# Seven-product chunks in five of eleven up-projection pairs, woven into one stream of units

## The chip, the cores and the metric

The kernel runs on one core of a Trainium2 chip. The metric is the device time of one execution in microseconds, as the median of several runs; lower is better. A core has a matrix engine (PE), a vector engine (DVE), a scalar engine (ACT), a third elementwise engine (POOL) and queues that issue transfers (SP's for most, POOL's for those that add to what lies at their target).

## The reference

A two-layer encoder over 256 positions of width 2048. Layer 0 mixes tokens by grouped-query attention, layer 1 by a dilated window attention; each is followed by a gated MLP. Only the MLP is touched:

```python
def conv_ffn(h, w_up, conv_w, conv_b, w_down):
    u = h @ w_up                      # [256, 2048] x [2048, 11264]
    ...
    u = lax.conv_general_dilated(...) + conv_b   # depthwise, width 3, over positions
    gate, val = jnp.split(u, 2, axis=-1)
    return (jax.nn.silu(gate) * val) @ w_down    # [256, 5632] x [5632, 2048]
```

Input and output are float32. The second mixer also needs tables of position biases, which the kernel writes to DRAM during the first MLP ("bias lines").

## The kernel before

**Products of float32.** A weight tile of 128x1024 is loaded raw, and split into a high part (`wh`, ACT, L130) and the rest (`wl`, DVE, L131); activations are kept split in the same way (`xh`, `xl`). A product is three matmuls: high by high, high by low, low by high. The 256 positions are two row halves m of 128; a matmul takes one 128x128 block of activations and 512 columns of weights.

**Units.** The up-projection has 11 pairs, each a block of 512 gate columns and the block of 512 value columns that belongs to it. The contraction of 2048 is four chunks (kg) of 512 rows. A plain unit `("c", kg, i)` is one raw tile: two row blocks of the weights, both row halves, three matmuls each, 12 in all. A chunk of a pair is four such units, two of gate and two of value, 48 matmuls. Alternatively a chunk is computed as a 2x2 block product with seven products in place of eight (Winograd's form of Strassen's method): a unit `("P", kg, f)` is one of the seven, 6 matmuls, 42 for the chunk. Its weight blocks are sums of raw tiles, its activations ("forms") sums of activation blocks, and the products M1, M5, M6, M7 have to be added up afterwards with the plain sums.

**The up-projection stage.** The MLP runs in two halves (`HALVES`: pairs 0 to 5, then 6 to 10); after each half the down-projection of these columns follows. All pairs but one run as plain feeds: `project` (L150s) computes the four gate chunks, then the four value chunks, and `feed` orders the matmuls of each activation block as `wh·xh`, `wl·xh`, `wh·xl`, so that the low part is wanted by the second matmul of a unit. Pair 0 goes through `project_woven`, which puts off the chunks whose activations come late and empties the list of waiting work before its ninth unit. Pair 6, the first of the second half, has chunk 0 by seven products through `seven` and `project_pair`, at its own start, one product and one plain unit in turn; its forms are made during the first down-projection (`first_half_forms`), and its weight sums are four DVE operations (L277). In `project_pair` a unit does its matmuls on the high part first and those on the low part last.

**Work around it.** After a block's sums are complete `up_post` scales them (ACT, L629), transposes them (DVE, L630), places the blocks (POOL, ACT, DVE: L395, L397, L399), applies the convolution's taps (ACT L638, DVE L642 and L644), and for a value block the product with the gate (L652, L668) and, in chunks that the down-projection computes by seven, the forms of the result (L684 to L696). It is a generator: `step()`, called after a unit, advances the first two of the pending ones by one stage. `spare` holds `bias_lines`, advanced when fewer than two are pending.

**Order on the engines.** A scheduler turns program order into one order per engine; a split is moved ahead by 45 instructions (`AHEAD`). There are six raw slots, three pairs of split buffers (`NHL`; the down-projection adds a fourth in `wh9`/`wl9`), and eight banks of sums: 0 to 3 in turn for a pair's gate and value, 4 to 7 for everything else (`ps_tile`, in turn).

Of the kernel before, what the change touches and what calls it, by code (L numbers as in the profile page):

```python
# [35 lines left out]
def tile_encoder(ctx: ExitStack, tc: tile.TileContext, x, xT, w_a, w_ao, q_gain, k_gain, w_b, w_bo,  # L36
# [25 lines left out]
    def nm(s):  # L62
        uid[0] += 1
        return f"{s}_{uid[0]}"
# [39 lines left out]
    def drain(keep=0):  # L104
        while len(pending) > keep:
            step()
# [110 lines left out]
    def project_pair(w, n0, n1, lhs, forms, units, late, early_done, n0_done, product_done=None, tail=False,  # L217
# [66 lines left out]
        for i, (kind, kg, p) in enumerate(units):  # L284
# [47 lines left out]
            if not (product_done or lazy) or kind == "c" or p in (1, 5, 7, 4):  # L332
                step()
        return acc

    def split(hi, lo, src):
        if lo is None:
# [91 lines left out]
    def make_forms(forms, src, k, tiles):  # L429
        for p, ms, k0 in ((1, slice(0, P), k), (2, slice(0, P), k + 2), (4, slice(P, NT), k + 2)):  # L430
            forms[p] = [tuple(t[:, ms] for t in src[k0 + j][:2]) for j in range(2)]
        yield
        xs, ts, fm = tiles()
        for j in range(4):
            hi, lo = src[k + j][:2]
            nc.vector.tensor_tensor(xs[:, j], hi.bitcast(F32), lo.bitcast(F32), ALU.add)
        yield
        q1, q0, q2, q4 = xs[:, :2, :P], xs[:, :2, P:], xs[:, 2:, :P], xs[:, 2:, P:]
        s3, s1, s2, s4 = (ts[:, i].rearrange("p (a t) -> p a t", a=2) for i in range(4))

# [12 lines left out]
        put(3, 3)  # L453
# [132 lines left out]
    def ffn(l, hT, ss_in, g_next, last, side=None):  # L586
        with tc.tile_pool(name=nm("wpool"), bufs=1) as wp, tc.tile_pool(name=nm("fpool"), bufs=1) as fp:
# [66 lines left out]
                for j in range(2):  # L654
                    split(*slots[k0 + j], cv[:, j, :])

            kept, first_forms = {}, {}

            def form_tiles():
                xs, ts = (t[:, :1024].rearrange("p (j c) -> p j c", j=4) for t in ut)  # L660
                return xs, ts, [fp.tile([P, 2, NT], F32R, tag=t, name=nm("fm"), bufs=3) for t in ("cg", "cg", "cv", "cv")]

            def first_half_forms():
                yield from make_forms(first_forms, hT, 0, form_tiles)
                zero_edges()

            def glu_forms(cg, cv, fm, hh):
                nc.vector.tensor_tensor(cv, cg, cv, ALU.mult)  # L668
# [29 lines left out]
                put(6, s2)  # L698
                put(3, s4)

            kgs = list(range(4))
            for hf, (p0, p1) in enumerate(HALVES):
                slots, forms = {}, {}
                tags = iter([(hpool, k) for k in range(24)] + [(wp, k) for k in range(24, 30)])
# [6 lines left out]
                for p in range(p0, p1):  # L711
                    if p - p0 in SKG[hf]:
                        fm = forms[p - p0] = {}
                        if p - p0 == 4:
                            f2 = fp.tile([P, 4, NT], F32R, tag="tT", name=nm("ff"))
                            f1 = fp.tile([P, 512], F32R, tag="junk", name=nm("ff"))
                            fm.update({7: (f2[:, 0], f2[:, 1]), 5: (f2[:, 2], f2[:, 3]), 6: (f1[:, :NT], f1[:, NT:])})
                        fm.update({f: new_form() for f in (1, 7, 2, 5, 4, 6, 3) + (0,) * hf if f not in fm})
                        if hf:
                            for kt in range(4):  # L720
                                slots[4 * (p - p0) + kt] = [
                                    tuple(t[:, kt % 2 * P:(kt % 2 + 1) * P] for t in fm[f])
                                    for f in ((1, 0), (2, 4))[kt // 2]]
                    else:
                        slots.update({4 * (p - p0) + j: new_form() for j in range(4)})
                    def new_tiles():
                        return ([fp.tile([P, 2, NT], F32, tag=t, name=nm(t), bufs=3) for _ in range(2)]
                                for t in ("cg", "cv"))

                    def after(hh, cg, cv, slots=slots, forms=forms, kg=p - p0):  # L730
# [4 lines left out]
                    if hf == 1 and p == p0:  # L735
                        sums = [wp.tile([P, 2, 512], F32, tag=t, name=nm("ms")) for t in ("wh9", "wl9")]
                        c = [("c", k, 2 * n + i) for n in range(2) for k in kgs[1:] for i in range(2)]
                        units = c[:2]
                        for i, f in enumerate(ORDER):
                            units += [("P", 0, f)] + c[2 + i:3 + i] * (i < 5)  # L740
                        units += c[7:]
                        cs = []

                        def gate_ready(a, p=p):
                            cs.extend(new_tiles())
                            start(up_post(a, p, cs[0]))

                        def value_ready(a, p=p, after=after):
                            start(up_post(a, NPAIR + p, cs[1], partial(after, cg=cs[0], cv=cs[1])))

                        seven(w_up[l], p, NPAIR + p, hT, lambda kg: first_forms, units,
                              [[t[:, i] for i in range(2)] for t in sums], gate_ready, value_ready)
                        continue
                    cg, cv = new_tiles()
                    after = partial(after, cg=cg, cv=cv)
                    if p == 0:
                        def gate_done(a, cg=cg):
                            taps()
                            start(up_post(a, 0, cg))

                        va = project_woven(w_up[l], p, NPAIR + p, hT, WOVEN, 4, gate_done)
                    else:
                        start(up_post(project(w_up[l], p, hT, kgs), p, cg))
                        va = project(w_up[l], NPAIR + p, hT, kgs)
                    start(up_post(va, NPAIR + p, cv, after))
# [362 lines left out]
    scr1 = dpool.tile([16, P, 256], F32, name="scr1")  # L1128

    def bias_lines(wp, lp):  # L1130
        if True:
            of = lp.tile([P, 2, 512], F32, tag="tT", name="of").rearrange("p a c -> p (a c)")
            oh = wp.tile([P, 1024], F32R, tag="wh9", name="oh")
            rb = lp.tile([P, 32], F32, name="rb")[:, :24]
            rs = lp.tile([P, 32], F32R, name="rs")[:, :24]
            nc.gpsimd.memset(rb, 0.0)
            nc.gpsimd.memset(rb[32:33, :], -1e30)
            for i in range(2):
                nc.gpsimd.dma_start(of[64 * i:64 * i + 64], onehot[:64])
                nc.gpsimd.dma_start(rb[64 * i:64 * i + 32, :], rel_bias)  # L1140
            yield
            yield
            lh = wp.tile([P, 24, 32], F32R, tag="wl9", name="lh")
            lnt = lp.tile([P, 2, 512], F32, tag="tT", name="lnt")
            nc.gpsimd.tensor_copy(rs, rb)
            nc.gpsimd.tensor_tensor(rs[64:], rb[64:], rs[64:].bitcast(F32), ALU.subtract)
            nc.gpsimd.tensor_copy(lh, rs.bitcast(F32)[:, :, None].to_broadcast([P, 24, 32]))
            nc.gpsimd.tensor_copy(oh, of)
            for b in range(6):
                for _ in range(2):  # L1150
                    yield
                c0, w = ((0, 512), (512, 256), (768, 256))[b // 2]
                t = ps_tile()
                nc.tensor.matmul(t[:, :w], lh[:, 4 * b:4 * b + 4, :].rearrange("p a r -> p (a r)"),
                                 oh[:, c0:c0 + w], start=True, stop=True)
                ln = lnt[:, b % 2]
                nc.vector.tensor_copy(ln[:, :w], t[:, :w])
                dst = scr0[4 * b:4 * b + 4] if b < 2 else scr1[4 * (b - 2):4 * (b - 2) + 4]
                for i in range(4):
                    yield  # L1160
                    nc.gpsimd.dma_start(dst[:, 32 * i:32 * i + 32, :], ln[:, :w])

    def mixer_b(hT, ss_in):
        with tc.tile_pool(name="bpool", bufs=1) as bp:
# [262 lines left out]
```

## Time and profile before

| | us |
|---|---|
| median of 3 runs | 2234.61 (2234.25 to 2234.72) |
| the profiled execution | 2234.03 |
| its span in the trace | 2232.2 |
| up-projections, layer 0, pairs 1 to 5 (window 308.4 to 526.3) | 217.9 |
| first down-projection, layer 0 (526.3 to 650.2) | 123.9 |
| pair 6 with its seven products (650.2 to 693.2) | 43.0 |

The page gives busy time per engine over the span. A window view gives the same for a stretch, with the number of instructions, the granted clock of PE (1.00 is full), the share of the DMA engines and their rate. A line of a group view has the line of the kernel, engine, operation, names of result and operands, shapes, count, then busy time, the mean duration in ns, and the idle time of the engine before these instructions with what ended it. A line of the timeline has start, duration, engine, line, operation. Wait lists give who waited for whom: total, count, longest.

### The profile page before, as it was taken

What the parts mean: (1) busy time and instruction counts of PE and PEld (TensorE: products, weight loads), DVE (VectorE), ACT (ScalarE), POOL (GpSimd) and SP (SyncE); (2) the same over time, 40 slices, a digit from 0 to 9 for tenths busy, and PEclk for the clock granted to TensorE, in tenths of its full rate; (3) what the DMA queues carried; (4) which work ended last, traced back from release to release, by engine and by line L of the source; (5) the groups of instructions that cost most, each with busy time, mean ns of one, the idle gap of its engine ahead of it and who ended that gap; (6) DMA issues with size and microseconds to landing.
All of it is one profiled execution on the core that took longest, in us unless ns stands there. A gap on an engine that the chain in (4) does not pass through costs nothing. (4 is left out here: it accounts for less than half of the span.)

```text
span 2232.2 us, 29276 instructions
## 1 busy us (share of the span) xinstructions
PE 2218.3 (99%) x9997; PEld 1834.7 (82%) x9997; DVE 1848.1 (83%) x2543; ACT 1564.8 (70%) x2411; POOL 349.1 (16%) x508
## 2 busy tenths in 40 slices
PE   9999999999999999999999999999999999999998
PEld 7888888888888888888888888888888888888886
DVE  6777778889998888879887978796887899888896
ACT  7665677777557777667876777575777765677764
POOL 2210212211001011111340213010111100011111
PEclk9999999999999999999999999999999999999999
DMA  8444657766776656766656565555666677566675
GB/s 302 163 148 151 204 189 210 242 200 193 235 217 205 199 193 193 246 204 205 214 176 191 167 207 179 189 197 185 196 193 194 199 226 227 199 197 191 222 236 161
DMA packets 129670, 448.99 MB, mean 201 GB/s; under 512 B 17664, under 2 KB 18432, under 8 KB 129520
## 3 DMA queue, kind: packets, MB, share of 16 engines
q1 hardware_dynamic: 119744, 425.64, 57.9%
q0 software_dynamic: 9344, 20.92, 4.9%
q8 instruction: 78, 1.28, 0.2%
q14 instruction: 72, 0.59, 0.1%
q10 hardware_dynamic: 432, 0.56, 0.1%
HBM read 438.11 MB, written 6.29 MB: 199 GB/s over the span
## 5 line engine op out<-in xcount | busy, mean ns | idle before, releaser
L131 DVE TENSOR_TENSOR wl<-raw,wh 128x1024 fp32r<-128x1024 f32 x873 | 1069.3, 1234 | 267.3 <-ACT wh L130 263.6
L130 ACT ACTIVATE wh<-raw 128x1024 fp32r<-128x1024 f32 x873 | 916.3, 1057 | 453.6 <-PE acc L157 157.6
L156 PE MATMUL acc<-wl,xh 128*128 128x512 f32 x1664 | 648.9, 390 | 1.4 <-DVE wl L131 0.9
L155 PE MATMUL acc<-wh,xh 128*128 128x512 f32 x1664 | 648.9, 390 | 0.5 <-ACT wh L166 0.5
L157 PE MATMUL acc<-wh,xh 128*128 128x512 f32 x1664 | 648.0, 389 | 0.0
L156 PEld LDWEIGHTS acc<-wl,xh 128*128 128x128 f32 x1664 | 312.5, 188 | 68.7 <-DVE wl L131 4.1
L155 PEld LDWEIGHTS acc<-wh,xh 128*128 128x128 f32 x1664 | 312.4, 188 | 64.7 <-ACT wh L166 0.9
L157 PEld LDWEIGHTS acc<-wh,xh 128*128 128x128 f32 x1664 | 312.4, 188 | 64.3
L320 PE MATMUL acc<-wh,ah 128*128 128x512 f32 x730 | 284.6, 390 | 0.4 <-DVE h L578 0.3
L322 PE MATMUL acc<-wh,al 128*128 128x512 f32 x730 | 284.3, 389 | 0.0
L395 POOL COPY u<-t 32x256 f32<-32x256 f32 x176 | 110.4, 627 | 805.3 <-DVE t L630 797.2
L325 PE MATMUL acc<-wl,ah 128*128 128x512 f32 x730 | 205.1, 390 | 0.6 <-DVE wl L131 0.6
L320 PE MATMUL acc<-wh,xh 128*128 128x512 f32 x416 | 162.9, 392 | 0.2 <-DVE h L578 0.2
L322 PE MATMUL acc<-wh,xh 128*128 128x512 f32 x416 | 162.0, 389 | 0.0
L320 PEld LDWEIGHTS acc<-wh,ah 128*128 128x128 f32 x730 | 137.0, 188 | 29.8 <-DVE h L578 1.3
L325 PEld LDWEIGHTS acc<-wl,ah 128*128 128x128 f32 x730 | 136.7, 188 | 30.2 <-DVE wl L131 2.0
L322 PEld LDWEIGHTS acc<-wh,al 128*128 128x128 f32 x730 | 137.1, 188 | 28.3
L397 ACT ACTIVATE u<-t 32x256 f32<-32x256 f32 x352 | 147.6, 419 | 17.2 <-DVE t L630 9.4
L325 PE MATMUL acc<-wl,xh 128*128 128x512 f32 x416 | 113.1, 390 | 0.0
L320 PEld LDWEIGHTS acc<-wh,xh 128*128 128x128 f32 x416 | 78.1, 188 | 16.8 <-DVE h L578 0.8
L325 PEld LDWEIGHTS acc<-wl,xh 128*128 128x128 f32 x416 | 78.0, 188 | 16.2
L322 PEld LDWEIGHTS acc<-wh,xh 128*128 128x128 f32 x416 | 78.1, 188 | 16.0
(271 smaller groups left out, 2487.1 us busy)
## 6 DMA issues: line engine op xcount, KB each, us to landing
raw<-in_w_up_dram SPq DMA_DIRECT2D x352, 512.0 KB, 4.5
raw<-in_w_down_dram SPq DMA_DIRECT2D x176, 512.0 KB, 5.0
raw<-in_w_b_dram SPq DMA_DIRECT2D x144, 512.0 KB, 4.5
raw<-in_w_bo_dram SPq DMA_DIRECT2D x48, 512.0 KB, 4.4
raw<-in_w_a_dram SPq DMA_DIRECT2D x40, 512.0 KB, 4.5
raw<-in_w_ao_dram SPq DMA_DIRECT2D x32, 512.0 KB, 3.7
raw<-in_w_down_dram POOLq DMA_DIRECT2D x17, 512.0 KB, 6.2
raw<-in_w_a_dram SPq DMA_DIRECT2D x16, 256.0 KB, 6.4
```

What stands on the lines that cost most here:

```text
L130: nc.scalar.activation(wh, r, AF.Copy)
L131: nc.vector.tensor_tensor(wl, r, wh.bitcast(F32), ALU.subtract)
L155: nc.tensor.matmul(accs[m], xh, wh[:, j, :], start=st, stop=False)
L156: nc.tensor.matmul(accs[m], xh, wl[:, j, :], start=False, stop=False)
L157: nc.tensor.matmul(accs[m], xl, wh[:, j, :], start=False, stop=sp)
L320: nc.tensor.matmul(acc[k], xh, wh[:, j, :], start=k in fresh, stop=False)
L322: nc.tensor.matmul(acc[k], xl, wh[:, j, :], start=False, stop=False)
L325: nc.tensor.matmul(acc[k], xh, wl[:, j, :], start=False, stop=last[k] == i and j == 1)
L395: nc.gpsimd.tensor_copy(dst, src)
L397: nc.scalar.activation(dst, src, AF.Copy)
```

## The change

All pairs of a half now run through one new function, `stream`, in place of `project`, `project_woven` and `seven`. It makes one list of units for the half. Pairs 1, 3, 5, 7 and 9 (`SEVEN_UP`) have their chunk 0 by seven products; these seven units are put into the preceding pair's last seven units, one after each (the last one after the pair's end), and the pair's own 12 plain units follow. Pair 6 is plain. In all units the matmuls on the high part come first. The seven-product pair's gate sums stay in the pair of banks whose turn it is; its value sums and M1, M5, M6, M7 take banks 4 to 7. The value sums take the banks of M1 and M5 once those are read.

Two of the four weight sums are made by transfers from POOL's queue that add to their target (`onto`: one reads the raw block from DRAM again, one reads a tile in SBUF); the other two stay on DVE. The forms are made at the start of each half (`half_forms`), in other tiles than before, and no longer in the down-projection. `bias_lines` uses other tiles, makes its left operand in six parts, has a matmul per 256 columns, and takes bank 7.

```diff
+SEVEN_UP = (1, 3, 5, 7, 9)
...
+    def stream(w, lhs, forms, pairs, is_seven, held, gate_done, value_done, new_sums):
+        units, left = [], {}
+        for p in pairs:
+            order = WOVEN if held and p == pairs[0] else [(c, k) for c in range(2) for k in range(4)]
+            if p in is_seven:
+                units[-7:] = [u for v, f in zip(units[-7:], ORDER_D) for u in (v, ("P", p, 0, f))]
+            units += [("c", p, k, 2 * c + i) for c, k in order for i in range(2) if k or p not in is_seven]
...
+        sets = [(bank_at[0] + 2) % 4, bank_at[0]]
...
+        def where(p, k):
+            if (p, k) not in acc:
+                n, m = {"11": (0, 0), "21": (0, 1), "12": (1, 0), "22": (1, 1)}.get(k, (None, None))
+                if n is None:
+                    i = {"M1": 4, "M5": 5, "M6": 6, "M7": 7}[k]
+                elif p in is_seven and n:
+                    i = 4 + m
+                else:
+                    i = sets[n] + m
...
+        def onto(b, src):
+            nc.gpsimd.dma_start(blocks[b].rearrange("p a c -> p (a c)"), src, accum_op=ALU.add)
+
+        def fetch(p, f):
+            if f == 1:
+                block(p, "11")
+                block(p, "12")
+            elif f == 2:
+                add("11", "12")
+                onto("12", w[p + NPAIR, 0][:, 1024:])
+            elif f == 5:
+                add("22", "11")
+                onto("21", block(p, "22").rearrange("p a c -> p (a c)"))
...
+        def product_done(p, f):
+            (k0, k1), (q0, q1) = sums[p]
+            k = {1: "M1", 5: "M5", 6: "M6", 7: "M7"}[f]
+            t = acc.pop((p, k))
+            if f in (1, 5):
+                nc.scalar.activation(k0 if f == 1 else q1, t, AF.Copy)
+            elif f == 6:
+                nc.vector.tensor_tensor(q0, t, k0, ALU.add)
+            else:
+                nc.vector.tensor_tensor(k1, t, q0, ALU.add)
+                nc.vector.tensor_tensor(q0, q0, q1, ALU.add)
+                nc.vector.tensor_tensor(q1, k1, q1, ALU.add)
+
+        for i, (kind, p, kg, f) in enumerate(units):
+            if held and i == 2 * held:
+                drain()
...
+            for t, fresh, xh, xl, j in todo:
+                nc.tensor.matmul(t, xh, wh[:, j, :], start=fresh, stop=False)
+                nc.tensor.matmul(t, xl, wh[:, j, :], start=False, stop=False)
...
+            for t, fresh, xh, xl, j in todo:
+                nc.tensor.matmul(t, xh, wl[:, j, :], start=False, stop=ends and j == 1)
+            if n is None:
+                product_done(p, f)
+            elif ends:
+                a = [acc.pop((p, k)) for k in (("11", "21"), ("12", "22"))[n]]
+                if p in is_seven:
+                    s = sums[p][n]
+                    for m in range(2):
+                        nc.vector.tensor_tensor(s[m], a[m], s[m], ALU.subtract if n else ALU.add)
+                    a = s
...
+                (gate_done, value_done)[n](a, p)
+            if kind == "c" or f in (1, 5, 7, 4):
+                step()
...
+            def half_forms(hf):
+                for _ in range(4 * hf):
+                    yield
+                yield from make_forms(up_forms[hf], hT, 0, partial(form_tiles, hf))
+                if hf:
+                    zero_edges()
...
+                start(half_forms(hf))
+                stream(w_up[l], hT, up_forms[hf], range(p0, p1), SEVEN_UP, 4 * (hf == 0), gate_done, value_done,
+                       lambda: [[t[:, i] for i in range(2)] for t in
+                                [wp.tile([P, 2, 512], F32, tag=t, name=nm("ms")) for t in ("wh9", "wl9")]])
...
-                if hf == 0:
-                    start(first_half_forms())
...
+        for b in range(6):
+            lh = lp.tile([P, 4, 32], F32R, tag="lh", name=nm("lh"), bufs=2)
+            nc.gpsimd.tensor_copy(lh, rs.bitcast(F32)[:, 4 * b:4 * b + 4, None].to_broadcast([P, 4, 32]))
...
+            cols = ((0, 1), (2,), (3,))[b // 2]
+            w = NT * len(cols)
+            t = bank(7, "ps")
+            for j, i in enumerate(cols):
+                nc.tensor.matmul(t[:, j * NT:(j + 1) * NT], lh.rearrange("p a r -> p (a r)"), oh[i],
+                                 start=True, stop=True)
```

More of the change, by code (lines that the diff above doesn't have):

```diff
@@ L334, in project_pair, with block, add @@
         return acc
+    def stream(w, lhs, forms, pairs, is_seven, held, gate_done, value_done, new_sums):
[5 more added lines that the diff above has]
+            units += [("c", p, k, 2 * c + i) for c, k in order for i in range(2) if k or p not in is_seven]
+            left.update({(p, n): 8 for n in range(2)})
+            if p in is_seven:
+                left.update({(p, 0): 8, (p, 1): 7})
+        sets = [(bank_at[0] + 2) % 4, bank_at[0]]
+        acc, sums, blocks = {}, {}, {}
+        def where(p, k):
[7 more added lines that the diff above has]
+                    i = sets[n] + m
+                acc[p, k] = bank(i, "acc")
+                return acc[p, k], True
+            return acc[p, k], False
+        def block(p, b):
+            if b not in blocks:
+                blocks[b] = load_raw(w, p + NPAIR * (int(b[1]) - 1), 0, int(b[0]) - 1)
+            return blocks[b]
+        def add(b, src):
+            with tc.high_priority(offset=AHEAD):
+                nc.vector.tensor_tensor(blocks[b], blocks[b], blocks[src], ALU.add)
+        def onto(b, src):
[10 more added lines that the diff above has]
+                onto("21", block(p, "22").rearrange("p a c -> p (a c)"))
+            b = {1: "11", 2: "21", 3: "22", 5: "11", 6: "22", 7: "12", 4: "21"}[f]
+            return b, block(p, b)
+        def product_done(p, f):
[13 more added lines that the diff above has]
+                drain()
+            if kind == "c":
+                b, r = None, load_raw(w, p + NPAIR * (f // 2), kg, f % 2)
+                n, ks = f // 2, (("11", "21"), ("12", "22"))[f // 2]
+            else:
+                b, r = fetch(p, f)
+                n = {2: 0, 4: 0, 3: 1}.get(f)
+                ks = ({1: "M1", 2: "11", 3: "12", 4: "21", 5: "M5", 6: "M6", 7: "M7"}[f],)
+                if f == 1:
+                    sums[p] = new_sums()
+            free = kind == "c" or f in (5, 6, 7, 4)
+            wh, wl = split_raw(r, free)
+            if kind == "P" and free:
+                blocks.pop(b)
+            todo = []
+            for j in range(2):
+                for m, k in enumerate(ks):
+                    if kind == "c":
+                        x = at(lhs[4 * kg + 2 * (f % 2) + j], m)
+                    else:
+                        x = forms[f]
+                        x = x[j] if isinstance(x, list) else [t[:, j * P:(j + 1) * P] for t in x]
+                    todo.append((*where(p, k), *x, j))
+            for t, fresh, xh, xl, j in todo:
+                nc.tensor.matmul(t, xh, wh[:, j, :], start=fresh, stop=False)
+                nc.tensor.matmul(t, xl, wh[:, j, :], start=False, stop=False)
+            todo.sort(key=lambda u: ([u[0] is acc[p, k] for k in ks].index(True), u[4]))
+            if n is not None:
+                left[p, n] -= 1
+            ends = n is None or left[p, n] == 0
+            for t, fresh, xh, xl, j in todo:
[4 more added lines that the diff above has]
+                a = [acc.pop((p, k)) for k in (("11", "21"), ("12", "22"))[n]]
+                if p in is_seven:
+                    s = sums[p][n]
+                    for m in range(2):
+                        nc.vector.tensor_tensor(s[m], a[m], s[m], ALU.subtract if n else ALU.add)
+                    a = s
+                    if n:
+                        sums.pop(p)
+                        sets.reverse()
+                (gate_done, value_done)[n](a, p)
+            if kind == "c" or f in (1, 5, 7, 4):
+                step()
+        bank_at[0] = sets[1]
@@ L655, in glu, with form_tiles @@
                     split(*slots[k0 + j], cv[:, j, :])
[L657 to L665, printed above, removed]
+            kept, up_forms = {}, ({}, {})
+            def form_tiles(hf):
+                fm = [tuple(wp.tile([P, NT], F32R, tag=f"a{c}{k}", name=nm("fm")) for c in "hl")
+                      for k in range(26 + 2 * hf, 30)]
+                if hf == 0:
+                    t = [wp.tile([P, 2, 512], F32, tag=t, name=nm("xs")).rearrange("p a c -> p (a c)")
+                         for t in ("wh9", "wl9")]
+                else:
+                    t = [t[:, :1024] for t in ut]
+                    f2 = fp.tile([P, 4, NT], F32R, tag="tT", name=nm("ff"))
+                    fm += [(f2[:, 0], f2[:, 1]), (f2[:, 2], f2[:, 3])]
+                return *(v.rearrange("p (j c) -> p j c", j=4) for v in t), fm
+            def half_forms(hf):
[4 more added lines that the diff above has]
+                    zero_edges()
             def glu_forms(cg, cv, fm, hh):
@@ L699, in glu_forms @@
                 put(3, s4)
-            kgs = list(range(4))
             for hf, (p0, p1) in enumerate(HALVES):
@@ L710, in ffn, with gate_done @@
                 wide.append(1)
-                for p in range(p0, p1):
+                cs = {}
+                def gate_done(a, p, hf=hf, p0=p0, slots=slots, forms=forms, new_form=new_form, cs=cs):
                     if p - p0 in SKG[hf]:
@@ L725, in ffn, with value_done, after @@
                         slots.update({4 * (p - p0) + j: new_form() for j in range(4)})
[L726 to L730, printed above, removed]
+                    if p == 0:
+                        taps()
+                    cs[p] = [[fp.tile([P, 2, NT], F32, tag=t, name=nm(t), bufs=3) for _ in range(2)]
+                             for t in ("cg", "cv")]
+                    start(up_post(a, p, cs[p][0]))
+                def value_done(a, p, p0=p0, slots=slots, forms=forms, cs=cs):
+                    cg, cv = cs.pop(p)
+                    def after(hh, kg=p - p0):
                         if kg in forms:
@@ L733, in after @@
                         return glu(cg[hh], cv[hh], slots, 4 * kg + 2 * hh)
[L735 to L765, printed above, removed]
+                    start(up_post(a, NPAIR + p, cv, after))
                     if p == 1 and side is not None:
                         spare.append(side(wp, fp))
+                start(half_forms(hf))
+                stream(w_up[l], hT, up_forms[hf], range(p0, p1), SEVEN_UP, 4 * (hf == 0), gate_done, value_done,
+                       lambda: [[t[:, i] for i in range(2)] for t in
+                                [wp.tile([P, 2, 512], F32, tag=t, name=nm("ms")) for t in ("wh9", "wl9")]])
                 def done(accs, n):
@@ L1130, in bias_lines @@
     def bias_lines(wp, lp):
[L1131 to L1161, printed above, removed]
@@ new lines, in bias_lines @@
+        of = lp.tile([P, 2, 512], F32, tag="tT", name="of").rearrange("p a c -> p (a c)")
+        oh = [wp.tile([P, NT], F32R, tag=f"a{c}{k}", name=nm("oh")) for k in (24, 25) for c in "hl"]
+        rb = lp.tile([P, 32], F32, name="rb")[:, :24]
+        rs = lp.tile([P, 32], F32R, name="rs")[:, :24]
+        nc.gpsimd.memset(rb, 0.0)
+        nc.gpsimd.memset(rb[32:33, :], -1e30)
+        for i in range(2):
+            nc.gpsimd.dma_start(of[64 * i:64 * i + 64], onehot[:64])
+            nc.gpsimd.dma_start(rb[64 * i:64 * i + 32, :], rel_bias)
```

15 lines of the change are left out of this document (added).

## The prediction

> **What bounds the kernel now.** I read the page's busy times first, then the same engines stage by stage, then the wait list of the stretch that the change rewrites.
>
> ```profile
> PE 2218.3 (99%) x9997; PEld 1834.7 (82%) x9997; DVE 1848.1 (83%) x2543; ACT 1564.8 (70%) x2411; POOL 349.1 (16%) x508
> ```
>
> TensorE (PE) works for 99% of the span; nothing else does. So the question for any edit is how many matmuls it takes away, and whether DVE or ACT then let PE starve. By stage (us, then busy time and count for PE, PEld, DVE, ACT, POOL; clock, DMA share, GB/s):
>
> ```profile
> core 0: us, PE busy (x) PEld busy (x) DVE busy (x) ACT busy (x) POOL busy (x), PEclk, DMA share, GB/s
> 264.70:308.40 43.70, 43.70 (x200) 36.14 (x199) 28.09 (x37) 28.10 (x40) 9.30 (x19) 1.00 0.64 196
> 526.30:650.20 123.90, 123.31 (x541) 101.11 (x540) 117.47 (x129) 76.91 (x90) 8.08 (x12) 1.00 0.75 224
> 650.20:693.20 43.00, 42.81 (x188) 34.99 (x188) 36.69 (x43) 26.36 (x35) 2.49 (x4) 1.00 0.60 198
> 693.20:737.40 44.20, 43.79 (x192) 35.41 (x191) 40.72 (x68) 35.63 (x60) 5.08 (x8) 1.00 0.57 187
> 868.50:920.00 51.50, 51.50 (x229) 42.62 (x228) 47.08 (x57) 35.65 (x48) 6.04 (x8) 1.00 0.78 230
> 974.40:1106.90 132.50, 132.50 (x608) 110.07 (x607) 118.44 (x141) 102.02 (x166) 31.06 (x44) 1.00 0.63 208
> 308.40:526.30 217.90, 217.90 (x965) 180.48 (x964) 182.62 (x283) 165.37 (x260) 41.51 (x64) 1.00 0.69 215
> ```
>
> These are, in layer 0: pair 0 of the up-projections; the first down-projection; pair 6 (the one with seven products today); pair 7; the start of the second down-projection; the first weave of mixer B; and pairs 1 to 5. In the last row five pairs of 192 matmuls (960) take 217.90 us: **0.227 us a matmul**, at granted clock 1.00 and without a gap. The same step stands between single starts:
>
> ```profile
> 352.54 0.39 PE L155 MATMUL acc<-wh,xh 128*128 128x512 f32 x1
> 352.77 0.39 PE L156 MATMUL acc<-wl,xh 128*128 128x512 f32 x1
> ```
>
> The 0.39 us is a latency; 0.227 is what one more matmul costs. Pairs 6 and 7 hold 186 and 192 matmuls, 85.8 us, but took 43.00 + 44.20 = 87.2: 1.4 us lost around the one seven. Most of that is a late low part, in pair 7:
>
> ```profile
> PEld acc L156 <- DVE wl L131: 1.5, 3, 0.8
> ```
>
> **What goes: matmuls.** A chunk of a pair is four units of 12 matmuls, 48; by seven products it is seven units of 6, 42. Today one pair a layer has that, afterwards five (1, 3, 5, 7, 9): four more, in two layers eight, 8 x 6 = 48 matmuls fewer. 48 x 0.227 = **10.9 us**, all of it on PE, which is the path. The TensorE page of the Trainium skill ("TensorE: Matmul & The Clock Gate", Back-to-back issue gap) gives N/2.4 + 2.5 ns, 216 ns for N=512, and about 131 ns for a sustained stream; 48 of these would be 10.4 or 6.3 us. The trace's stream runs at 227 ns, so I keep to the row.
>
> The bias lines turn two 512-wide matmuls into four 256-wide ones, in layer 0: between 0 and 2 x 0.227 = 0.45 us. The columns are the same, so I take 0. Their bank is now fixed (7), which the seventh product also uses: a bias matmul behind it waits for one DVE read, one 0.68 us operation (below) and what stands before it; I put that into the stall term.
>
> **What is added on DVE and ACT.** Rows for the costs, over pairs 1 to 5 and for today's seven:
>
> ```profile
> L131 DVE TENSOR_TENSOR wl<-raw,wh 128x1024 fp32r<-128x1024 f32 x82 | 101.3, 1235 | 28.0 <-ACT wh L130 27.4
> L399 DVE COPY u<-t 32x256 f32<-32x256 f32 x40 | 14.5, 362 | 1.3
> L630 DVE STREAM_TRANSPOSE t<-s 128x512 f32<-128x512 f32 x20 | 14.1, 706 | 2.5 <-ACT s L629 2.5
> L644 DVE SCALAR_TENSOR_TENSOR cv<-u,cw,cv 128x256 f32<-128x256 f32 x20 | 9.6, 482 | 0.4
> L341 DVE TENSOR_TENSOR al<-cv,ah 128x256 fp32r<-128x256 f32 x17 | 6.8, 419 | 0.0
> L668 DVE TENSOR_TENSOR cv<-cg,cv 128x512 f32<-128x512 f32 x6 | 4.1, 688 | 0.1
> L277 DVE TENSOR_TENSOR raw<-raw,raw 128x1024 f32<-128x1024 f32 x40 | 49.3, 1234 | 2.3 <-DMA raw<-in_w_up_dram 1.8
> L420 DVE TENSOR_TENSOR ms<-acc,ms 128x512 f32<-128x512 f32 x8 | 5.5, 684 | 0.0
> L130 ACT ACTIVATE wh<-raw 128x1024 fp32r<-128x1024 f32 x873 | 916.3, 1057 | 453.6 <-PE acc L157 157.6
> L412 ACT ACTIVATE ms<-ps 128x512 f32<-128x512 f32 x24 | 13.9, 578 | 0.0
> ```
>
> Each seven adds to DVE three splits (3 x 1.235), two block sums (2 x 1.234) and eight 128x512 sums (8 x 0.684): 11.6 us by duration. To ACT: 3 x 1.057 + 2 x 0.578 = 4.3 us. But durations overcount a full queue, as the DVE timeline shows:
>
> ```profile
> 694.08 1.22 DVE L131 TENSOR_TENSOR wl<-raw,wh 128x1024 fp32r<-128x1024 f32 x1
> 695.22 0.88 DVE L642 SCALAR_TENSOR_TENSOR cg<-u,cw,cg 128x256 f32<-128x256 f32 x2
> 696.80 0.68 DVE L425 TENSOR_TENSOR ms<-acc,ms 128x512 f32<-128x512 f32 x1
> 697.40 0.68 DVE L426 TENSOR_TENSOR ms<-acc,ms 128x512 f32<-128x512 f32 x1
> ```
>
> A split of 1.22 us is followed after 1.14, a 0.68 sum after 0.60: about 0.08 of each overlaps the next one. Now the stretch that is hardest: seven products woven into the last seven units of the preceding pair (126 matmuls, 28.6 us), then the seven's own 12 units (144, 32.7 us), together 61.3 us of PE. DVE there: 26 splits x 1.14 = 29.6, two block sums 2.3, eight sums x 0.60 = 4.8, three post-processings (two transposes x 0.63, four copies x 0.40 (0.36 and the gap between two), eight taps x 0.40: 6.1 each) 18.2, and the GLU with its forms (pairs 0, 2, 4, 6, 8 all have them) 2 x 0.60 + 11 x 0.34 = 4.9. Sum **59.8 of 61.3 us**; by full durations the same list is 66.2. The nine plain units ahead of it have slack: 9 x 1.14 + 6.1 + 2.5 = 18.9 of 24.5.
>
> So DVE is nearly full for 61 us, and PE has to live on three split buffers. The nearest rows: the first down-projection, a denser weave with four buffers, ran DVE at 117.47 of 123.90 us and PE lost 0.6; the second (47.08 of 51.50) and mixer B (118.44 of 132.50, three buffers, as here) lost nothing. Against that stands pair 6 with 1.4 us. There the loss came afterwards, in plain feeds, where the second matmul of a unit already wants the low part; in the stream a plain unit does eight matmuls on the high part first, 8 x 0.227 = 1.8 us later, and the waits listed were 0.8 at most. A stall per seven thus lies between 0 and 1.4 us; I take 0.2, near the weaves that have the same order: 10 x 0.2 = **+2.0**. In layer 1 the same stretch (pair 6, then pairs 7 to 10) is
>
> ```profile
> 1901.00:1943.70 42.70, 42.70 (x189) 35.04 (x188) 36.37 (x42) 26.42 (x35) 2.49 (x4) 1.00 0.58 196
> 1943.70:2118.90 175.20, 174.79 (x770) 143.88 (x769) 147.43 (x227) 135.42 (x215) 22.07 (x36) 1.00 0.63 201
> ```
>
> 954 matmuls, 216.6 us, in 217.9: 1.3 lost. What pair 6 loses today, 1.4 + 1.3, goes with its seven, but for some 0.3 to 0.4 a layer that I put to the change of stage: **-2.0**.
>
> **What I cost at nothing.** The forms are made in each half, not once a layer: 12 DVE operations x 0.42 = 5.0 us and four ACT copies. In pair 0 they lie in the slack of the first row above (DVE 28.09 of 43.70). In the second half they leave the down-projection, where DVE was at 95%, and go to pair 6, which loses its own seven; without that cover they would cost up to 5 us twice. Each seven also issues two transfers from POOL in place of DVE sums, twenty in all:
>
> ```profile
> raw<-in_w_up_dram SPq DMA_DIRECT2D x352, 512.0 KB, 4.5
> raw<-in_w_down_dram POOLq DMA_DIRECT2D x17, 512.0 KB, 6.2
> raw<-raw POOLq DMA_DIRECT2D x5, 512.0 KB, 6.6
> 870.00 2.77 POOL L395 COPY u<-t 32x256 f32<-32x256 f32 x4 [17.44 <-DVE t L630]
> 875.98 0.86 POOL L251 DMA_DIRECT2D raw<-in_w_down_dram  x1 [3.20 <-ACT wh L130]
> 884.41 0.86 POOL L251 DMA_DIRECT2D raw<-raw  x1 [7.57 <-DVE raw L255]
> ```
>
> The later one is issued at product 5 and used at product 4, with three products and three plain units between: 3 x 1.36 + 3 x 2.72 = 12.2 us, less about 4 by which splits run ahead, against 0.86 + 6.6. It just fits. While it waits for its DVE sum, POOL's copies of the next post-processing queue behind it, and ACT's taps behind those; but the gate's copies are issued a unit before the transfers and the value's come after the last unit, 12 us later. On SP nothing is added: a chunk is four loads either way, and during the weave two of six raw slots carry the plain loads, each turned round in 8.2 us (two plain units and two products) against 4.5 to landing; mixer B's weave lives on the same two.
>
> Sum: -10.9 + 2.0 - 2.0 = -10.9. The profiled execution took 2234.03 us (span 2232.2 and 1.8 around it), 0.6 under the median of 2234.61; so **2223.7 us** for the median.
>
> **Rivals.** (a) *The loss of pair 6 repeats at every seven.* 10 x 1.4 = 14 in place of 2, and the old 2.0 gone: 2235.7, no difference. For it: same stage, and DVE at 40.72 of 44.20 in pair 7. Against: the order within units above, and weaves without loss. Chance 0.10. (b) *DVE becomes the engine that paces the stretch: slower.* If DVE's operations did not overlap, the list takes 66.2 us; three buffers cover one plain unit (2.7), so 66.2 - 61.3 - 2.7 = 2.2 us a seven, 22 in all, less 10.9 and 2.0: 2243.7. It makes the kernel slower from 65.7 us on (2.7 covered, and 1.7 a seven to eat the gain and 0.2%). Against it: 1.14 between starts, not 1.22, and DVE at 95% in the first down-projection with PE fed. Chance 0.08. The VectorE page of the Trainium skill ("VectorE: DVE Perf Modes", The DRAIN you can't avoid) says that the next operation doesn't start until the pipe has emptied; that would make this rival. The rows at 694 to 697 us show starts before the end of the one before. (c) *All cover holds and more goes*: no stall at the sevens, and the first down-projections, freed of the forms, lose their 0.6 each: 2234.6 - 10.9 - 2.0 - 1.2 = 2220.5; a part of the forecast. That the matmuls don't go isn't a case: their count follows from the unit lists.
>
> **How the numbers follow.** Forecast with (c): 0.82, for stalls of 0 to 0.8 us a seven, 2220.5 to 2229.7. (a) 0.10, (b) 0.08. The range 2220.5 to 2230 leaves out (a) and (b), 0.18. A measurement tells 0.2% (4.5 us) from no change: faster 0.82, same 0.10, slower 0.08.
>
> **What would show it.** PE's matmuls fall by 46 (48 fewer, two narrow ones more). Pairs 0 and 1 together (378 matmuls) last 85.8 us if the sevens are free. Right: PE idle under 0.5 us in the weave, DVE above 90% there. Wrong: waits of the matmuls on DVE's wl or ACT's wh in a seven's 12 units, of more than 0.8 us a seven; ACT waiting for the raw<-raw landing in time for product 4; POOL's copies late behind the transfers.

## The result and the profile after

The changed kernel takes 2257.68 us (median of 4 runs, 2255.74 to 2259.22) against 2234.66 (4 runs, 2234.25 to 2235.33) for the kernel before beside it: ratio 1.0102, 95% interval 1.0085 to 1.012. It is 1% slower; 2223.7 us, 0.5% faster, was predicted. The profiled execution took 2259.22 us, the slowest of the four; its span is 2257.4.

The page's busy line after the change (share of the span, then the number of instructions):

```profile
PE 2222.6 (98%) x9951; PEld 1830.3 (81%) x9951; DVE 1923.5 (85%) x2667; ACT 1581.1 (70%) x2457; POOL 384.8 (17%) x536
```

The matmuls did go: 9951 records against 9997, the 46 fewer that were announced. Yet PE is busy 4.3 us longer, not 10.9 less, so its matmuls have become slower by some 15 us in all; and the span has grown by 25.2 us, so PE idles about 21 us more. Both need a place. The six up- and down-projection stages that matter, in the window view of the kernel before, with the cuts laid at the stages' ends (columns as in the prediction):

```profile
262.80:526.30 263.50, 263.50 (x1171) 218.20 (x1170) 212.32 (x321) 195.13 (x302) 50.81 (x83) 1.00 0.68 211
526.30:650.30 124.00, 123.41 (x542) 101.18 (x541) 117.57 (x129) 77.01 (x90) 8.08 (x12) 1.00 0.75 224
650.30:868.30 218.00, 217.41 (x955) 178.72 (x954) 184.09 (x269) 161.59 (x248) 23.11 (x36) 1.00 0.61 197
1514.80:1777.20 262.40, 262.40 (x1164) 217.24 (x1163) 209.35 (x315) 194.32 (x302) 29.69 (x49) 1.00 0.61 194
1777.20:1901.10 123.90, 123.51 (x542) 101.18 (x541) 118.00 (x130) 77.34 (x90) 8.05 (x12) 1.00 0.75 225
1901.10:2118.80 217.70, 217.29 (x956) 178.76 (x955) 183.69 (x268) 161.65 (x248) 24.56 (x40) 1.00 0.62 200
```

and of the kernel after:

```profile
263.40:535.60 272.20, 265.77 (x1155) 216.16 (x1154) 237.90 (x362) 201.58 (x319) 63.94 (x97) 0.98 0.70 213
535.60:669.30 133.70, 127.55 (x542) 103.27 (x541) 124.53 (x139) 78.23 (x90) 8.87 (x11) 0.97 0.72 217
669.30:885.20 215.90, 215.69 (x950) 177.78 (x949) 189.86 (x281) 162.37 (x254) 28.36 (x41) 1.00 0.65 205
1531.60:1791.60 260.00, 259.65 (x1146) 213.52 (x1145) 234.51 (x356) 201.28 (x319) 38.75 (x55) 1.00 0.65 204
1791.60:1926.10 134.50, 127.78 (x541) 102.98 (x540) 124.87 (x140) 78.73 (x90) 8.84 (x11) 0.97 0.72 219
1926.10:2142.10 216.00, 215.75 (x950) 177.84 (x949) 189.58 (x280) 162.47 (x254) 29.99 (x45) 1.00 0.67 208
```

In order: layer 0's first-half up-projection, first down-projection, second-half up-projection, then the same of layer 1. The differences are +8.7, +9.7, -2.1, -2.4, +10.6, -1.7: 22.8 of the 25.2 us; most of the rest, 1.9 us, came in layer 1's second down-projection (113.4 to 115.3) and was not followed. Three stages became faster, about as foreseen. Three became slower, and two of those are down-projections, of which the change rewrote nothing but the forms that left them. The waits of PE over the whole run of after, longest groups (total, times, longest), name the two kinds of stall; before, no such group of the up- or down-projections was above 0.9 us in total:

```profile
PE acc L326 <- DVE wl L132: 8.3, 5, 2.9
PE acc L427 <- ACT wh L131: 6.4, 4, 5.6
PE acc L321 <- ACT wh L131: 5.4, 3, 2.3
```

L321 and L326 are the down-projection's matmuls, L427 the stream's.

**The door of the down-projection.** The timeline of after, layer 0, PE:

```profile
542.31 1.20 PE L326 MATMUL acc<-wl,ah 128*128 128x512 f32 x4 [2.93 <-DVE wl L132]
543.34 0.39 PE L321 MATMUL acc<-wh,ah 128*128 128x512 f32 x1
543.57 0.59 PE L323 MATMUL acc<-wh,al 128*128 128x512 f32 x1
543.96 0.63 PE L321 MATMUL acc<-wh,ah 128*128 128x512 f32 x1
544.39 0.63 PE L323 MATMUL acc<-wh,al 128*128 128x512 f32 x1
```

PE waits 2.93 us for a low part and then starts a matmul every 0.43 us in place of 0.227. The same microseconds on DVE, and on ACT:

```profile
536.10 2.35 DVE L132 TENSOR_TENSOR wl<-raw,wh 128x1024 fp32r<-128x1024 f32 x2
538.38 0.41 DVE L552 TENSOR_TENSOR u<-xh 128x256 f32<-128x256 f32 x1
538.71 1.28 DVE L442 TENSOR_TENSOR ms<-acc,ms 128x512 f32<-128x512 f32 x2
539.91 2.35 DVE L132 TENSOR_TENSOR wl<-raw,wh 128x1024 fp32r<-128x1024 f32 x2
```

```profile
539.42 1.33 ACT L745 ACTIVATE s<-ms,rstd 128x512 f32<-128x512 f32 x2 [1.62 <-DVE ms L442]
```

The two sums at 538.71 are pair 5's value sums; they lie in the tile `wl9`, and ACT reads them until 540.75. The down-projection's fourth split buffer is `wh9`/`wl9`, put first in its ring (L943). Two causes lie in this picture: the buffer that isn't free (**A**), and DVE, without a gap in these rows, coming out of pair 5's seven with work still queued (**B**). In layer 1 the same wait stands at 1795. A second stall follows in both layers (2.33 and 1.98 us), in layer 0 here:

```profile
579.89 0.50 PE L321 MATMUL acc<-wh,ah 128*128 128x512 f32 x1 [2.33 <-ACT wh L131]
```

ACT had itself waited 5.2 us there, for a block of weights to which POOL's queue was adding (issued at 570.0, landed at 577.7), so what came last here was a transfer and not DVE. In the run with both edits below the same wait is 0.7 us in each layer; it seems to hang on the delay at the door.

**The stores of the bias lines.** In the first half of layer 0 the worst stall is elsewhere (PE's timeline and one window, after):

```profile
400.88 0.80 PE L427 MATMUL acc<-wh,xh 128*128 128x512 f32 x1 [5.61 <-ACT wh L131]
```

```profile
394.50:407.00 12.50, 6.85 (x17) 5.17 (x18) 3.96 (x5) 5.01 (x6) 0.29 (x1) 0.59 0.85 247
```

17 matmuls in 12.5 us, 3.9 us of work. This is the weave of pair 3. Just ahead of it POOL issues, and the transfers issued from 383 to 396 take (KB each, median us to landing):

```profile
385.39 2.72 POOL L1269 DMA_DIRECT2D scr<-lnt  x4
393.51 0.95 POOL L373 DMA_DIRECT2D raw<-raw  x1 [5.40 <-issue]
```

```profile
raw<-in_w_up_dram SPq DMA_DIRECT2D x3, 512.0 KB, 10.8
scr<-lnt POOLq DMA_DIRECT2D x4, 256.0 KB, 14.0
raw<-raw POOLq DMA_DIRECT2D x1, 512.0 KB, 11.2
```

Plain loads that landed in 4.5 us as a rule took 10.8 beside four stores of 256 KB to DRAM. One of them, issued at 387.18, took 12.5; it landed at 399.67, and ACT began the split for the matmul of 400.88 at 399.77:

```profile
raw<-in_w_up_dram SPq DMA_DIRECT2D x1, 512.0 KB, 12.5
```

Two controls come free. The same weave in layer 1, which has no bias lines (issues of 1649 to 1662; window):

```profile
raw<-in_w_up_dram SPq DMA_DIRECT2D x4, 512.0 KB, 5.4
```

```profile
1644.00:1660.50 16.50, 16.50 (x73) 13.45 (x73) 15.75 (x24) 13.40 (x23) 5.09 (x6) 1.00 0.65 183
```

And the same stores in the kernel before, among plain units (issues of 383 to 396; window):

```profile
raw<-in_w_up_dram SPq DMA_DIRECT2D x5, 512.0 KB, 9.9
scr<-lnt POOLq DMA_DIRECT2D x4, 256.0 KB, 10.8
```

```profile
383.00:396.00 13.00, 13.00 (x59) 10.78 (x58) 9.92 (x14) 8.62 (x11) 2.68 (x4) 1.00 0.88 227
```

PE lost nothing in either: the weave alone runs, and slow loads alone are covered by six raw slots. Together, with four of the six slots held by the seven's blocks (as the program has it), they stop PE. This is theory **C**. Layer 1's first half lost 1.7 us against its matmuls (262.4 - 18 x 0.227 = 258.3; it took 260.0), layer 0's 12.8 (263.5 - 4.1 = 259.4; 272.2), so C would be worth about 11 us.

### The profile page after: what moved, and what is told of

The parts are those of the page before. It is cut to its first block, busy times and chain, and to the rows that moved or that the text cites. A ratio compares the mean times of both kernels' runs of the same rounds, so it can differ in the third digit from the quotient of the medians.

```text
span 2257.4 us, 29504 instructions
## 1 busy us (share of the span) xinstructions
PE 2222.6 (98%) x9951; PEld 1830.3 (81%) x9951; DVE 1923.5 (85%) x2667; ACT 1581.1 (70%) x2457; POOL 384.8 (17%) x536
## 5 line engine op out<-in xcount | busy, mean ns | idle before, releaser
L132 DVE TENSOR_TENSOR wl<-raw,wh 128x1024 fp32r<-128x1024 f32 x897 | 1089.3, 1228 | 240.8 <-ACT wh L131 231.4
L131 ACT ACTIVATE wh<-raw 128x1024 fp32r<-128x1024 f32 x897 | 934.8, 1055 | 457.3 <-PE acc L323 116.7
L427 PE MATMUL acc<-wh,xh 128*128 128x512 f32 x1308 | 512.0, 391 | 6.5 <-ACT wh L131 6.4
L428 PE MATMUL acc<-wh,xh 128*128 128x512 f32 x1308 | 510.2, 390 | 0.0
L434 PE MATMUL acc<-wl,xh 128*128 128x512 f32 x1308 | 353.4, 390 | 0.5 <-DVE wl L132 0.2
L427 PEld LDWEIGHTS acc<-wh,xh 128*128 128x128 f32 x1308 | 246.1, 188 | 61.8 <-ACT wh L131 10.7
L321 PE MATMUL acc<-wh,ah 128*128 128x512 f32 x730 | 287.5, 394 | 5.4 <-ACT wh L131 5.4
L434 PEld LDWEIGHTS acc<-wl,xh 128*128 128x128 f32 x1308 | 245.8, 188 | 53.2 <-DVE wl L132 2.0
L428 PEld LDWEIGHTS acc<-wh,xh 128*128 128x128 f32 x1308 | 246.2, 188 | 50.8
L511 POOL COPY u<-t 32x256 f32<-32x256 f32 x176 | 122.1, 694 | 638.4 <-DVE t L746 630.3
L326 PE MATMUL acc<-wl,ah 128*128 128x512 f32 x730 | 207.4, 394 | 7.7 <-DVE wl L132 7.6
L326 PEld LDWEIGHTS acc<-wl,ah 128*128 128x128 f32 x730 | 137.7, 190 | 39.6 <-DVE wl L132 11.1
L321 PEld LDWEIGHTS acc<-wh,ah 128*128 128x128 f32 x730 | 138.6, 190 | 35.9 <-ACT wh L131 6.7
L156 PE MATMUL acc<-wh,xh 128*128 128x512 f32 x384 | 150.2, 393 | 1.1 <-ACT wh L167 1.1
L157 PE MATMUL acc<-wl,xh 128*128 128x512 f32 x384 | 150.3, 391 | 1.1 <-DVE wl L168 0.8
L158 PE MATMUL acc<-wh,xh 128*128 128x512 f32 x384 | 150.0, 391 | 0.0
L321 PE MATMUL acc<-wh,xh 128*128 128x512 f32 x312 | 122.2, 392 | 0.0
L323 PE MATMUL acc<-wh,xh 128*128 128x512 f32 x312 | 121.5, 389 | 0.0
L157 PEld LDWEIGHTS acc<-wl,xh 128*128 128x128 f32 x384 | 72.2, 188 | 16.7 <-DVE wl L168 1.6
```

The source lines that it names most:

```text
L131: nc.scalar.activation(wh, r, AF.Copy)
L132: nc.vector.tensor_tensor(wl, r, wh.bitcast(F32), ALU.subtract)
L156: nc.tensor.matmul(accs[m], xh, wh[:, j, :], start=st, stop=False)
L157: nc.tensor.matmul(accs[m], xh, wl[:, j, :], start=False, stop=False)
L158: nc.tensor.matmul(accs[m], xl, wh[:, j, :], start=False, stop=sp)
L321: nc.tensor.matmul(acc[k], xh, wh[:, j, :], start=k in fresh, stop=False)
```

## The experiments

Single runs are compared with each other and with the kernel before on the same chip (2233.5 for the first seven, 2234.1 for the last two). The changed kernel's own four executions lie within 3.5 us, so a difference of less than that between single runs says little by itself. The stages of a run are set against the trace of the changed kernel, its slowest execution.

**No seven in pair 5.** Does the loss in the down-projections belong to that seven at all?

```diff
-SEVEN_UP = (1, 3, 5, 7, 9)
+SEVEN_UP = (1, 3, 7, 9)
```

> Pair 5, the last of the first half, is computed plainly (sevens at 1, 3, 7, 9): 12 matmuls more, +2.7 us. Theory A (the first down-projection starves because the last seven ends at its door: its value sums lie in the wh9/wl9 tiles that the down-projection's first unit splits into, and everything late there follows from that): the stalls in the first down-projections of both layers go, about 10 us each; 2257.7 - 20 + 2.7 = 2240. Theory B (the first down-projection starves from the DVE work that ten sevens leave behind): it keeps most of its stalls, 2255 to 2260. Under both the 5.8 us stall at 395 us of layer 0 stays.

2238.72 us (one run). The windows of the first half and of the first down-projections of both layers:

```profile
262.70:533.50 270.80, 265.65 (x1160) 216.38 (x1160) 233.52 (x359) 200.24 (x316) 62.03 (x95) 0.99 0.70 214
533.50:658.80 125.30, 123.61 (x542) 101.08 (x541) 117.06 (x127) 75.63 (x88) 8.84 (x11) 1.00 0.74 224
1782.70:1907.10 124.40, 123.22 (x542) 101.28 (x541) 117.66 (x128) 76.15 (x88) 8.74 (x11) 1.00 0.75 229
```

133.7 and 134.5 became 125.3 and 124.4: the down-projections lost their time to pair 5's seven, all but about 1 us. DVE's work in them fell by 7 us, back to before's 117: that is what the seven had left over for them. The first half keeps 10.0 of its 12.8 us (263.5 - 12 x 0.227 = 260.8; it took 270.8), as C has it, though not in one stall: PE waited there four times, 0.56 to 1.65 us, from 386 to 399.

**The fourth buffer last in the ring.** This takes A away and leaves the seven and DVE's load.

```diff
-                hl_ring.insert(0, (wp, 9))
+                hl_ring.append((wp, 9))
```

> All sevens stay; the down-projection takes the fourth split buffer (wh9/wl9) as its last in turn and not as its first. Theory A: the 3.1 us stalls at the start of the two first down-projections and the half clock behind them (1.6 us each) go, and what is late after them too: about 20 us, 2237.5. Theory B: only the start's 4.7 us a layer go, the stalls 40 us later (2.5 and 2.1 us and their half clock) stay: 2248.

2252.3 us (one run), slower than both expectations. The down-projections, and the longest wait of PE that is left there in layer 0:

```profile
534.10:664.70 130.60, 124.96 (x542) 100.69 (x541) 124.37 (x141) 78.18 (x91) 8.67 (x11) 1.00 0.74 223
1789.10:1919.10 130.00, 125.76 (x542) 102.09 (x541) 124.88 (x142) 79.23 (x92) 8.64 (x11) 0.99 0.75 225
```

```profile
560.44 0.73 PE L326 MATMUL acc<-wl,ah 128*128 128x512 f32 x2 [2.11 <-DVE wl L132]
```

The wait at the door is gone, 3.1 and 4.5 us with it. But DVE is as full as it was, and PE now runs into it a little later. A is real and is the smaller part: 6.6 and 6.1 us above the kernel before remain.

**Bias lines a pair earlier.** The stores of 256 KB then fall before pair 3's weave; some of 128 KB still meet it.

```diff
-                    if p == 1 and side is not None:
+                    if p == 0 and side is not None:
```

> The bias lines start one pair earlier, after pair 0, so that their two 256 KB blocks are stored during pair 1's plain units and not during the weave of pair 3. Theory C (the 5.8 us stall at 395 us of layer 0 and the half clock after it come from the bias stores, behind which a raw load took 12.5 us while the weave left only two raw slots): no stall of over 1 us in the weaves, 2257.7 - 11 = 2246. Rival (the two raw slots and the transfers from POOL starve the weave anyway): the stall stays in place, 2256 to 2259.

2254.95 us (one run), between the two. The first half of layer 0:

```profile
262.40:528.20 265.80, 262.29 (x1155) 214.01 (x1154) 237.03 (x362) 201.49 (x319) 64.63 (x97) 1.00 0.71 218
```

272.2 became 265.8: the long stall is gone, and waits of at most 1.1 us remain, at pair 1's units and in pair 3's weave. So C is right for that stage, and the edit worth 6.4 us there. The total fell by only 2.7 from the median, 4.3 from the profiled execution: the down-projections took 135.2 and 136.1 us, 1.5 more each. For that no cause was found; in layer 1 the edit changes nothing, so it may be spread between executions.

**Both edits**, the ring's order and the early bias lines.

> The ring's order of e2 and the start of the bias lines of e3 together. A and C: 2257.7 - 20 - 11 = 2227, faster than before by 0.3%. B and C: 2237, no difference from before.

2246.70 us (4 runs, 2246.42 to 2248.26), ratio 1.006, interval 1.0043 to 1.0077. Neither sum of theories was reached. The down-projections (131.9 and 129.2 us):

```profile
528.90:660.80 131.90, 126.53 (x542) 101.89 (x541) 123.15 (x140) 78.22 (x91) 8.67 (x11) 0.99 0.72 219
1783.80:1913.00 129.20, 124.62 (x542) 100.84 (x541) 124.49 (x142) 78.67 (x92) 8.65 (x11) 1.00 0.74 226
```

**DVE relieved, the seven kept.** On top of both edits, the two outer taps of pair 5's convolution are left out, 16 DVE operations of 0.40 us a layer. If B is right, the down-projections must get faster although nothing about buffers, banks or transfers changes.

```diff
-                    for j in range(2):
+                    for j in range(0 if n % NPAIR == 5 else 2):
                         cj, uj = halves(c[:, j]), u[:, 2 * hh + j]
```

> As e4_both, but the convolution's outer two taps are left out for pair 5 (16 DVE operations of 0.40 us a layer, 6.4 us, just ahead of and at the start of the first down-projection); the result isn't the reference's there. If it is DVE's work that the seven of pair 5 pushes over the door of the down-projection (theory B, now in front), the stalls in the first 30 us of both first down-projections (together some 10 us in e4_both) fall under 3: 2246.7 - 8 = 2238 or less. If something else holds it (a bank, a buffer, the transfers), they stay: 2245 to 2248.

2240.01 us (one run). The down-projections:

```profile
531.20:657.30 126.10, 123.87 (x542) 100.97 (x541) 118.25 (x125) 78.09 (x91) 8.68 (x11) 1.00 0.75 229
1780.80:1907.80 127.00, 124.26 (x542) 100.73 (x541) 119.42 (x127) 78.18 (x91) 8.65 (x11) 1.00 0.77 230
```

5.8 and 2.2 us off, for 5 us less work on DVE in the stage. The total is 2 us above what B had asked for and 5 below the alternative, so B holds: DVE's 123 to 125 us of work held PE back there. Not all of the difference is DVE's work alone: in layer 0 a stretch of half clock (described further down), worth some 1.7 us, went with the wait in front of it. At 118 and 119 us of work the stage is still 2.1 and 3.1 us longer than before.

**Pairs 2 and 4 in place of 1, 3 and 5.** No seven at the door, and the weaves at other times.

```diff
-SEVEN_UP = (1, 3, 5, 7, 9)
+SEVEN_UP = (2, 4, 7, 9)
```

> Sevens at 2, 4, 7, 9 instead of 1, 3, 5, 7, 9; nothing else changed. Pair 4's seven is followed by plain pair 5, and the two 256 KB blocks of the bias lines (371 to 388 us) fall among plain units. B and C: no stall of over 1.5 us from 260 us on, 2238.7 of e1 less its 7 us at 385 to 400: 2232, no difference from before. If a seven in the first half costs as such (its bunching, not its place): 2238.

2235.41 us (10 runs, 2232.14 to 2237.73), ratio 1.0009, interval 0.9999 to 1.0018; the 2232 was missed. The reason is C once more: four stores of 128 KB meet pair 4's weave (issues of 424 to 440, and the window behind them):

```profile
raw<-in_w_up_dram SPq DMA_DIRECT2D x4, 512.0 KB, 7.1
scr<-lnt POOLq DMA_DIRECT2D x4, 128.0 KB, 9.6
```

```profile
437.50:447.00 9.50, 6.47 (x22) 5.08 (x22) 5.07 (x6) 5.14 (x6) 0.85 (x2) 0.82 0.86 225
```

22 matmuls in 9.5 us, 5.0 us of work. One load, issued at 429.9, took 9.5 us, and PE waited 3.0 us behind it. So half the store size can be enough, but it need not be: with the early bias lines, four stores of 128 KB issued at 387.7 met pair 3's weave too, the load issued among them at 390.1 took 7.3 us, and no wait there was above 1.1 us.

**No seven in pair 5 and early bias lines** (the edits of the first and the third experiment).

> e1_no5 with the bias lines started after pair 0. If the two causes add: 2238.7 - 6 = 2232.7. If the bias lines only move the loss (their matmuls wait for bank 7, their stores meet pair 1's and pair 2's loads): 2236.

2234.43 us (10 runs, 2232.9 to 2237.43), ratio 1.0003, interval 0.9993 to 1.0013: between the two expectations. The first half of layer 0 took 268.7 us, only 2.1 less than with the first edit alone: shifted by a pair, the stores meet pair 1's plain units and pair 3's weave, and PE waits in smaller pieces, 1.1 us at the longest.

**Sevens where nothing else is**: layer 0's second half, and layer 1 without pair 5.

```diff
-SEVEN_UP = (1, 3, 5, 7, 9)
+SEVEN_UP = ((7, 9), (1, 3, 7, 9))
...
-                start(half_forms(hf))
-                stream(..., SEVEN_UP, ...
+                if any(p in SEVEN_UP[l] for p in range(p0, p1)):
+                    start(half_forms(hf))
+                stream(..., SEVEN_UP[l], ...
```

> Sevens where neither cause acts: layer 0 (with the bias lines) at 7 and 9 alone, layer 1 at 1, 3, 7, 9. 24 matmuls fewer than before, -5.4 us; layer 0's first half should look as before with its bias lines, and no weave is followed by a down-projection. B and C: before less 5 us, 2228.5. If the stream itself (its order, its one list) costs, also without sevens in a half: 2232 to 2236.

2233.16 us (11 runs, 2231.87 to 2235.93) against 2234.13 (21 runs), ratio 0.9998, interval 0.9989 to 1.0007. The first halves of both layers:

```profile
262.70:526.40 263.70, 263.70 (x1173) 218.33 (x1173) 208.22 (x321) 194.00 (x302) 55.40 (x91) 1.00 0.67 211
1514.70:1776.20 261.50, 260.85 (x1152) 214.76 (x1151) 230.11 (x353) 199.79 (x316) 36.08 (x53) 1.00 0.64 202
```

In layer 0 the stores are there and the weaves aren't: 263.7 us, all of it PE at work. With before, layer 1 and the changed kernel the square is complete: stores alone lose nothing, weaves alone some 2 us, both together 12.8. But 24 matmuls fewer are 5.4 us, and the medians differ by 1.0, which the interval doesn't tell from nothing. The 2228.5 of B and C was missed; the result lies in the range for a cost of the stream itself. Two sevens save 2.7 us in layer 1's first half and lose 1.8 of it, and the first down-projections stay at 124.8 and 124.9, about 1 us above before, in layer 0 behind a first half without any seven.

**Only the second halves.** As above with `SEVEN_UP = ((7, 9), (7, 9))`.

> Only 7 and 9 in both layers: 12 matmuls fewer than before, -2.7 us, and the 2 us that pair 6 loses today gone: 2229 to 2231. If sevens in layer 1's first half (e8) cost more than they save, this one is the faster of the two.

2233.93 us (10 runs, 2233.32 to 2236.62), ratio 1.0, interval 0.9991 to 1.0009, above the 2229 to 2231 expected. No version beat the kernel before by more than can be measured.

## Why the prediction was wrong

**Right: the matmuls.** 46 records fewer. In the stages where nothing else interferes their price of 0.227 us came off.

**Right in kind, mis-sized: the stall per seven, "I take 0.2".** The weave is nearly full on DVE and PE survives it. The second halves hold 5 x 192 - 12 = 948 matmuls, 215.2 us, and took 215.9 and 216.0: 0.35 to 0.4 a seven. Layer 1's first half lost 1.7 in three, 0.57 each. For ten sevens that is 3.5 to 5.7 us in place of 2.0.

**Right: what was costed at nothing**, as far as layer 1's first half and the second halves can show: forms in each half, POOL's accumulating transfers in time for product 4, POOL's copies behind them. The loss of pair 6 went, too.

**Wrong: "DVE there: ... Sum 59.8 of 61.3 us".** The stretch was cut off too early. For pair 5 of layer 1 it looked as forecast, DVE above 90% and PE without a gap; the same length of plain units before stands above it:

```profile
308.40:369.70 61.30, 61.30 (x272) 50.79 (x271) 52.25 (x83) 46.83 (x75) 9.79 (x15) 1.00 0.62 197
1730.20:1791.60 61.40, 61.40 (x271) 50.61 (x270) 56.93 (x87) 49.58 (x79) 10.32 (x14) 1.00 0.69 213
```

A seven adds 11.6 us of DVE work, by the prediction's own rows. Only 4.7 of them were done inside the stretch (56.93 - 52.25); the other 6.9 turn up in the down-projection behind it (124.87 against 118.00). Ahead of the stretch lie nine plain units with slack; behind it, for pairs 1, 3, 7 and 9, plain units that absorb what is left over. Pair 5 is the last of its half. Behind it comes the down-projection, whose DVE time of 117.47 in 123.90 us was quoted in the prediction, as a reason to expect no trouble. The 7 us of left-over work met 6 us of slack spread over 124 us. Nor was it asked who owns `wh9`/`wl9` at that moment, which the diff and the ring show. The two cost 9.7 and 10.6 us; the buffer's part is 3.1 to 4.5 by the ring experiment, and taking 5 us of DVE work away gave back 2.2 to 5.8 more. What remains is in part the 1 us that is open below. Rival (b) had the right engine, but charged each seven instead of the two at the doors.

**Wrong: "On SP nothing is added ... each turned round in 8.2 us ... against 4.5 to landing".** 4.5 is a median over the whole run. Beside the bias lines' stores a load took 10.8 (before: 9.9, in the kernel that I had the trace of), more than the 8.2 that two slots allow. I costed the bias lines by their matmuls and bank alone; their transfers, 24 on POOL's queue, were not new, but the slots that had covered them were given to the weave. About 11 us in layer 0 by comparison with layer 1, of which moving the stores by a pair gave back 6.4.

**Left out: the price of a stall.** I counted stalls by their length. Here five of them are followed by matmuls at half rate: for 6.2 us behind the 5.6 us, and for 3.4 us each behind 2.93, 2.33, 2.94 and 1.98 us. Half of these 20 us, some 10 us by this estimate, comes on top of the idle time; it is the larger part of the 15 us by which PE's work grew, and the rest has not been placed. The last of the five, and a stretch of the first experiment behind idle times of 0.79 and 1.65 us that ended at 396.81 and 399.20:

```profile
1837.20:1840.70 3.50, 3.50 (x10) 2.72 (x9) 3.50 (x4) 1.24 (x3) 0.00 (x0) 0.51 0.75 245
397.00:404.00 7.00, 5.35 (x16) 3.94 (x16) 3.61 (x4) 5.01 (x6) 0.00 (x0) 0.76 0.98 254
```

The Trainium skill ("TensorE: Matmul & The Clock Gate", Part 1: The HAM clock gate) says that the clock falls to half after an idle window of about 3.4 us and stays so until about 3.4 us of work, with 427 ns between matmuls of 512 columns. The trace agrees on the interval, 0.43 us, and on some 3.4 us at half clock; but the drop came here after idle times well below 3.4 us, down to the 1.98 and 1.65 us just shown.

The pieces add up: 10.9 of matmuls gained; 20.3 lost at the doors, 11 to the stores and some 5 at the sevens, with 2.0 of the old loss gone: +23, as between the medians. The losses are read from the stages, so this sum shows that nothing large is missing and is no test of the causes.

**Still open**: why the first down-projections stay about 1 us slower without a seven at the door. It is no seven's work: with sevens in the second halves alone they took 124.4 and 125.7 us, and PE waits on low parts for 1.2 and 1.5 us in them, against 0.3 in layer 0 before. Open, too, is why they moved by 1.5 us where only the bias lines did. Stores of the bias lines in another layout, or spread over layer 0, were not tried.

## What to carry to other kernels

A stretch that fills an engine has to be followed to the first place with slack behind it: ask what the next stage needs of that engine, and which buffers it expects to be free at its door. A landing time is not one number: take it from the moment in question, with the other transfers of that moment, before giving up the slots that hid it. And a stall of PE can cost more than its length: here some that lasted 1.65 us and more did, so look at the granted clock behind each.

## What the runs showed of the hardware

Behind some of PE's idle times the granted clock was 0.50 and matmuls started every 0.43 us: for some 3.4 us behind 1.98, 2.33, 2.93 and 2.94 us after the change, behind 0.79 and 1.65 us close together without a seven in pair 5, and behind 1.70, 2.20 and 3.21 us with the early bias lines; for 6.2 us behind 5.6 us. At 542.3 and 579.9 the drop came only some 1.3 us after the restart. The length of the idle time alone does not decide: with the early bias lines PE went on at its full rate after 2.73 and 2.57 us (at 1793.1 and 1830.8), and in the ring experiment it did so after 2.11 us (at 560.4) but not after 2.10 (at 1815.7). Four stores of 256 KB doubled the landing of 512 KB loads beside them, 4.5 to 9.9 or 10.8 us, while all queues together moved 227 (before) and 209 GB/s (after) from 383 to 396; four of 128 KB took it to 7.1 (7.5 in the run with the early bias lines).
